# A hybrid token-mixer block on one core: PSUM copies on ScalarE, attention's end and projection reordered, S5 outputs in column halves, the first norm's chain reordered

## The chip, the cores and the metric

The kernel runs on one core of a Trainium2 chip. The metric is device time in microseconds of one execution; the figures are medians over several executions. TensorE (PE) multiplies matrices and writes to PSUM, VectorE (DVE) and ScalarE (ACT) read PSUM and SBUF and compute element by element, GpSimd (POOL) does small fills, and the SyncE queue (SP) issues most DMAs.

## The reference

One decoder layer on x of shape (1, 512, 1024). Two sub-layers, each with an RMS norm, a scale and shift made from c (adaLN), a second norm and a gated residual:

```python
mod = silu(c) @ ada_w + ada_b
sh1, sc1, gt1, sh2, sc2, gt2 = split(mod, 6)
h = rms_norm(x, pre1_w) * (1 + sc1) + sh1
gq, gk, gv, ga, gr, mq, mk, mv, mi, mf, mo, su, zg = split(h @ w_in)
y_gla = rms_norm(gla(gq, gk, gv, log_sigmoid(ga @ a2 + b) / 16)) * silu(gr)
y_ml  = sigmoid(mo) * mlstm(silu(causal_dwconv([mq, mk])), mv, mi, mf)
y_s5  = gelu(s5(su)); y_s5 = y_s5 * sigmoid(y_s5 @ glu_w + glu_b)
y = (g0 * (y_gla @ proj_gla) + g1 * (y_ml @ proj_ml) + g2 * (y_s5 @ proj_s5)) @ w_out
x = x + (1 + gt1) * rms_norm(y, post1_w)
h = rms_norm(x, pre2_w) * (1 + sc2) + sh2
a, b = split(h @ ffn_in); x = x + (1 + gt2) * rms_norm((silu(a) * b) @ ffn_out, post2_w)
```

`gla` is gated linear attention (4 heads, key width 64, value width 128), `mlstm` a matrix memory with a stabiliser, and `s5` a diagonal complex state-space layer: 32 groups of 16 channels, 64 states each, y = Re(C x_t) + D u_t.

## The kernel before

Each weight matrix is streamed once and split into a rounded part `hi` (ScalarE, `af`, L229) and a remainder `lo` (VectorE, `tt`, L220). A product is then three matmuls, hi·hi, hi·lo and lo·hi, of 128x128 weights and 512 columns (`passes`, L422 to L424; `tok_mm`, L1526 to L1528; `slab0`, L1608 to L1610). Activations lie feature by token (`hT`), 8 tiles of 128 features.

- **Head** (0 to 66 us, from L534). The engines keep the order in which it is written (`manual_schedule`). Squares of x are summed by one-column matmuls (L556); from them comes r, one factor for each token. `rd` is the identity scaled by r (L569), and `rb`, a matmul of ones with it (L573), lays r out along the free axis. adaLN comes from `ada_pe` (L485), matmuls on column tiles of 32; `evac` copies their sums (`ae`), `prep` turns them into columns `cb` (L593) and builds `hT`, then the `sweep` multiplies six 128-column slabs of the input projection over five STRIPS of features. `warm` (L541) issues matmuls whose result nobody uses.
- **Attention** (66 to 190 us). Outside the manual stretches a scheduler moves instructions of different engines, so the order written is not always the order run. `log_sig` makes decays with ACT's Abs, Exp and Ln; `level` (L1087) runs 14 times; `kdT` and `Sg` carry the state from chunk to chunk; `og` is the output, scaled by `rg` and `gr`; `to_fm` (L1200) transposes it in 16 matmuls. `fill(n)` interleaves n steps of independent projection matmuls.
- **S5** (190 to 316 us). For each of four blocks `params` builds CA, WT and M, `states` the carried states Xs, and `outputs` (L1313) multiplies M by U and CA by Xs (L1318, L1319): 128x128 weights and 64 columns, in 8 groups. The scheduler mixes DVE's pieces of one block with splits (`lo`) for the projections that fill PE.
- mLSTM (to 405 us) and the branch projections follow.
- **Out-projection** (to 562 us, manual from L1628). `half(t, h)` projects 128 tokens on 512 columns; `gated`, `normed`, `x1_out`, `second` are the second norm and the residual; `to_h2` (L1580) transposes the result; `slab0` is the first slab of the feed-forward for one token tile. The feed-forward runs to 908 us.

## Time and profile before

| | us |
|---|---|
| median of 3 runs (910.48 to 912.75) | 912.28 |
| profiled execution | 910.4 |
| its span | 908.6 |
| PE busy (98% of the span) | 888.7 |
| DVE busy (63%) | 575.7 |
| ACT busy (36%) | 331.0 |

The profiled execution is 1.8 us longer than its span and 1.9 us below the median. The share of the span is an average: the stages have different limits, so a wait of PE is looked up in its own stage. The granted clock of PE over the whole execution was 0.989 of full speed.

### The profile page before, as it was taken

How to read it: one execution, taken by the hardware profiler on the slowest of the kernel's cores; microseconds unless marked ns; L12 is line 12 of the kernel's file. 1: busy time of each engine (PE TensorE's matmuls, PEld its weight loads, DVE VectorE, ACT ScalarE, POOL GpSimd, SP SyncE). 2: the span in 40 equal slices, each digit the busy share in tenths (PEclk: the TensorE clock that was granted, in tenths of full speed). 3: DMA queues.
4: the chain of work that ended last, by engine and by line, in shares of the span. 5: the costliest groups of instructions: out<-in, count | busy, mean ns of one | idle time of the engine just before them, and what ended most of it. 6: DMA issues, size and time to landing. Idle time of an engine off the chain costs nothing.

```text
span 908.6 us, 11582 instructions
## 1 busy us (share of the span) xinstructions
PE 888.7 (98%) x4334; PEld 723.1 (80%) x4334; DVE 575.7 (63%) x1144; ACT 331.0 (36%) x512; POOL 24.9 (3%) x68
## 2 busy tenths in 40 slices
PE   9999999999989999999999989999999999999997
PEld 7667887878878878788888868888888888888885
DVE  6748999979879884966679497544433333322215
ACT  4339323431442462722334444333222332211113
POOL 2010000000000000010000000000000000000000
PEclk7999999999999999999999999999999999999999
DMA  9661341233443442345456533533333323322303
GB/s 364 251 193 47 116 128 58 82 125 111 154 139 108 121 116 93 131 127 172 153 175 226 199 140 117 185 116 117 118 126 130 113 93 116 115 93 97 113 1 139
DMA packets 52193, 120.79 MB, mean 133 GB/s; under 512 B 13797, under 2 KB 19429, under 8 KB 52137
## 3 DMA queue, kind: packets, MB, share of 16 engines
q1 hardware_dynamic: 49944, 115.92, 38.0%
q0 software_dynamic: 1040, 2.38, 1.1%
q10 hardware_dynamic: 1152, 1.75, 0.5%
q8 instruction: 34, 0.56, 0.3%
q14 instruction: 23, 0.18, 0.1%
HBM read 113.21 MB, written 6.82 MB: 132 GB/s over the span
## 4 chain that ended last, share of the span: by engine, by line
PE 77%; DVE 17%; issue 2%; ACT 2%; DMA 1%; SPq 0%; DVEq 0%; ACTq 0%
PE mm L422 16%; PE mm L423 16%; PE mm L424 16%; PE y L1527 5%; PE y L1526 5%; PE y L1528 5%; DVE lo L220 3%; PE mm L455 2%; PE mm L454 2%; PE mm L456 2%; DVE ST L1111 1%; DVE Qp L220 1%; DVE o L220 1%; DVE D L220 1%; PE ax L1318 1%
## 5 line engine op out<-in xcount | busy, mean ns | idle before, releaser
L229 ACT ACTIVATE hi<-raw 128x1024 fp32r<-128x1024 f32 (+2 forms) x157 | 151.9, 971 | 382.2 <-PE mm L423 156.2
L220 DVE TENSOR_TENSOR lo<-raw,hi 128x1024 fp32r<-128x1024 f32 (+2 forms) x157 | 174.6, 1114 | 155.6 <-ACT hi L229 155.0
L424 PE MATMUL mm<-h2hi,lo 128*128 128x512 f32 x320 | 124.6, 389 | 0.0
L423 PE MATMUL mm<-h2lo,hi 128*128 128x512 f32 x320 | 124.6, 389 | 0.0
L422 PE MATMUL mm<-h2hi,hi 128*128 128x512 f32 x320 | 124.5, 389 | 0.0
L424 PE MATMUL mm<-hT,lo 128*128 128x512 f32 x280 | 110.7, 395 | 3.1 <-DVE lo L220 3.1
L422 PE MATMUL mm<-hT,hi 128*128 128x512 f32 x280 | 112.3, 401 | 0.2 <-ACT hT L229 0.2
L423 PE MATMUL mm<-hT,hi 128*128 128x512 f32 x280 | 111.0, 396 | 0.4 <-DVE hT L226 0.4
L422 PEld LDWEIGHTS mm<-h2hi,hi 128*128 128x128 f32 x320 | 60.1, 188 | 12.5
L424 PEld LDWEIGHTS mm<-h2hi,lo 128*128 128x128 f32 x320 | 60.1, 188 | 12.4
L423 PEld LDWEIGHTS mm<-h2lo,hi 128*128 128x128 f32 x320 | 60.1, 188 | 12.3
L1528 PE MATMUL y<-hi,g 128*128 128x512 f32 x176 | 68.5, 389 | 0.0
L1527 PE MATMUL y<-lo,g 128*128 128x512 f32 x176 | 68.5, 389 | 0.0
L1526 PE MATMUL y<-hi,g 128*128 128x512 f32 x176 | 68.3, 389 | 0.0
L220 DVE TENSOR_TENSOR sg<-sg,mm 128x512 f32<-128x512 f32 x36 | 24.7, 685 | 64.8 <-PE mm L424 64.7
L422 PEld LDWEIGHTS mm<-hT,hi 128*128 128x128 f32 x280 | 53.2, 190 | 15.7 <-issue 4.0
L424 PEld LDWEIGHTS mm<-hT,lo 128*128 128x128 f32 x280 | 53.2, 190 | 14.6 <-DVE lo L220 3.5
L423 PEld LDWEIGHTS mm<-hT,hi 128*128 128x128 f32 x280 | 53.1, 190 | 11.9 <-DVE hT L226 1.2
L226 DVE SCALAR_TENSOR_TENSOR gacc<-raw,cact,gacc 128x512 f32<-128x512 f32 x56 | 41.9, 748 | 21.9 <-DMA raw<-ada 21.3
L455 PE MATMUL mm<-lo,hT 128*128 128x512 f32 x128 | 50.5, 394 | 0.4 <-DVE lo L220 0.4
L454 PE MATMUL mm<-hi,hT 128*128 128x512 f32 x128 | 49.8, 399 | 0.0
L456 PE MATMUL mm<-hi,hT 128*128 128x512 f32 x128 | 49.7, 391 | 0.0
(311 smaller groups left out, 1393.9 us busy)
## 6 DMA issues: line engine op xcount, KB each, us to landing
raw<-ada SPq DMA_DIRECT2D x48, 512.0 KB, 3.5
raw<-ffn SPq DMA_DIRECT2D x44, 512.0 KB, 3.3
raw<-wzg SPq DMA_DIRECT2D x24, 512.0 KB, 3.2
raw<-ffo SPq DMA_DIRECT2D x22, 512.0 KB, 3.3
raw<-wpr SPq DMA_DIRECT2D x24, 256.0 KB, 2.7
raw<-wout SPq DMA_DIRECT2D x8, 512.0 KB, 4.3
raw<-sweep SPq DMA_DIRECT2D x8, 384.0 KB, 8.5
xT<-xT SPq DMA_DIRECT2D x4, 512.0 KB, 5.6
```

Source lines behind the costliest of these rows:

```text
L220: e.tensor_tensor(out=o, in0=a, in1=b, op=op)
L226: dve.scalar_tensor_tensor(out=o, in0=a, scalar=s, in1=b, op0=op0, op1=op1)
L229: act.activation(out=o, in_=i, func=f, **kw)
L422: mm(ps, lhsT=whi, rhs=xhi, start=first, stop=False)
L423: mm(ps, lhsT=whi, rhs=xlo, start=False, stop=False)
L424: mm(ps, lhsT=wlo, rhs=xhi, start=False, stop=last)
L454: mm(ps[t], lhsT=xh[:, tk], rhs=hi[:, sl], start=(k == 0), stop=False)
L455: mm(ps[t], lhsT=xh[:, tk], rhs=lo[:, sl], start=False, stop=False)
L456: mm(ps[t], lhsT=xl[:, tk], rhs=hi[:, sl], start=False, stop=(k == 7))
L1526: mm(ps, lhsT=xhi, rhs=whi[:, sl], start=first, stop=False)
L1527: mm(ps, lhsT=xhi, rhs=wlo[:, sl], start=False, stop=False)
L1528: mm(ps, lhsT=xlo, rhs=whi[:, sl], start=False, stop=last)
```

## The change

The copies out of PSUM named `gk`, `su`, `kdT` and `ks`, and the first term of the causal convolution, go from VectorE to ScalarE. In attention, the output of the first token tile is multiplied before the loop that makes Sg, and `og` is scaled head by head. S5's outputs take U and Xs as 64-column weights in alternating column halves, with M and CA streamed as 128 columns; the result comes out turned round, so four transposes a block and one more copy follow. In the head, `ae` and the columns stand ahead of `rd`, `rd` is split between the two engines, the first `lo` stands behind `h`, the first strip runs all hi·hi matmuls before the others, and there are 8 more warm matmuls behind the first 18. In the out-projection `half(3, 1)` stands between `to_h2(0)` and `to_h2(1)`, and `to_h2(2)` in the middle of `slab0(1)`.

```diff
...
-WARM = (17, 1, 0, 0, 0, 0)
+WARM = (17, 1, 1, 2, 2, 3)
-SWN = ((0, 0, 2), (0, 2, 3), (2, 4, 6), (2, 4, 6))
+SWN = ((0, 1, 2), (0, 2, 3), (2, 4, 6), (2, 4, 6))
...
+        def step_hi(self):
+            i = self.done
+            t, w = self.raw.pop(i), items[i]["w"]
+            hp, lp = self.rings[3]
+            hi = hp.tile([128, w], F32R, tag="hi", name="hi")
+            lo = lp.tile([128, w], F32R, tag="lo", name="lo")
+            af(hi, t[:, 0:w], AF.Copy)
+            self.hl[i] = (hi, lo)
+            self.done += 1
+            return lambda: tt(dve, lo, t[:, 0:w], hi.bitcast(F32), OP.subtract)
...
     cp(cz[:, :, 0:1], cact.unsqueeze(2))
     wb = ax_bank()
-    def warm(n, x):
+    def warm(n, x, bank=None):
         for _ in range(n):
-            mm(wb[:, 0:128], lhsT=ones, rhs=x, start=True, stop=True)
+            mm((bank or wb)[:, 0:128], lhsT=ones, rhs=x, start=True, stop=True)
...
+    ada_sb, cbs = {}, {}
+    def evac(j):
+        n = 2 * STRIPS[j][1]
+        ada_sb[j] = slot("ae")
+        af(ada_sb[j][:, 0:n], ada_ps.pop(j)[:, 0:n], AF.Copy)
+    def columns(j):
+        cbs[j] = cb = ax_bank()
+        for i in range(2 * STRIPS[j][1] // 128):
+            sl = slice(i * 128, (i + 1) * 128)
+            mm(cb[:, i:i + 1], lhsT=ada_sb[j][:, sl], rhs=ones[:, 0:1], start=True, stop=True)
+    evac(0)
+    columns(0)
     rb = ax_bank()
     rd = slot("rd")
     for t in range(4):
         tk = slice(t * 128, (t + 1) * 128)
-        af(rd[:, tk], ident, AF.Copy, scale=r[:, t:t + 1])
+        if t % 2:
+            af(rd[:, tk], ident, AF.Copy, scale=r[:, t:t + 1])
+        else:
+            ts(dve, rd[:, tk], ident, r[:, t:t + 1], None, OP.mult)
+    for t in range(4):
+        tk = slice(t * 128, (t + 1) * 128)
         mm(rb[:, tk], lhsT=ones, rhs=rd[:, tk], start=True, stop=True)
...
+    first_lo = S.step_hi()
...
-        cb = ax_bank()
-        for i in range(2 * n):
-            sl = slice(i * 128, (i + 1) * 128)
-            mm(cb[:, i:i + 1], lhsT=ada_sb[j][:, sl], rhs=ones[:, 0:1], start=True, stop=True)
+        if j not in cbs:
+            columns(j)
+        cb = cbs.pop(j)
...
+        if j == 0:
+            first_lo()
...
+            if k == 0:
+                yield
+                xhi, xlo = hT[k]
+                for n, (w, x) in enumerate(((hi, xhi), (lo, xhi), (hi, xlo))):
+                    for b in range(6):
+                        mm(sweep_ps[b], lhsT=w[:, b * 128:(b + 1) * 128], rhs=x, start=(n == 0), stop=False)
+                    yield
+                continue
...
-            ts(dve, u, ps, w(3), P("conv_b", f), OP.mult, OP.add)
+            af(u, ps, AF.Identity, scale=w(3), bias=P("conv_b", f))
...
-            cp(u.rearrange("p (a n) -> p a n", a=8)[:, ::-1], ps.rearrange("p (n a) -> p a n", a=8))
+            af(u.rearrange("p (a n) -> p a n", a=8)[:, ::-1], ps.rearrange("p (n a) -> p a n", a=8), AF.Copy)
...
-        S.ahead(strip_w[0][-1], 0)
         prep(0)
-        warm(WARM[5], ones)
...
+                if j == 0 and n == 0:
+                    warm(WARM[5], ones, sweep_ps[0])
...
-        cp(kT[p], sweep_ps[2 + p])
+        af(kT[p], sweep_ps[2 + p], AF.Copy)
...
-        cp(kdT[p][:, 0:384], ps[:, 0:384])
+        af(kdT[p][:, 0:384], ps[:, 0:384], AF.Copy)
     FL.until("gv")
     fill(2)
...
     og = {}
     ssg, rg = st3[:, 16:32], st3[:, 32:48]
-    for t in range(4):
+    def gla_out(t):
...
+    gla_out(0)
+    for p in range(2):
...
+    for t in range(1, 4):
+        gla_out(t)
     rstd(rg, ssg, 16, 128.0)
     FL.until("gr")
-    for t in range(4):
-        for h in range(4):
+    for h in range(4):
+        for t in range(4):
...
-        cp(ks[:, 0:256], kp[:, 0:256])
+        af(ks[:, 0:256], kp[:, 0:256], AF.Copy)
...
     def outputs(b):
         ps = ax_bank()
-        for g in range(8):
-            o = ps[:, g * 64:(g + 1) * 64]
-            sl = slice(g * 128, (g + 1) * 128)
-            mm(o, lhsT=Mt[b][:, sl], rhs=U[b][:, g * 64:(g + 1) * 64], start=True, stop=False)
-            mm(o, lhsT=CA[b][:, sl], rhs=Xs[b][:, g * 64:(g + 1) * 64], start=False, stop=True)
-        Y = slot("Y")
-        af(Y, ps, AF.Gelu_apprx_tanh)
+        half = (even, odd)
+        for q in range(4):
+            for z, (x, w) in enumerate(((U[b], Mt[b]), (Xs[b], CA[b]))):
+                for h in range(2):
+                    g = 2 * q + h
+                    mm(ps[half[h], q * 128:(q + 1) * 128], lhsT=x[:, g * 64:(g + 1) * 64],
+                       rhs=w[:, g * 128:(g + 1) * 128], start=(q == 0 and z == 0), stop=(q == 3 and z == 1),
+                       tile_position=(0, 64 * h))
+        YT, Y = slot("YT"), slot("Y")
+        af(YT, ps, AF.Gelu_apprx_tanh)
+        fill(1)
+        ps = ax_bank()
+        for q in range(4):
+            pe.transpose(out=ps[:, q * 128:(q + 1) * 128], in_=YT[:, q * 128:(q + 1) * 128], identity=ident)
+        af(Y, ps, AF.Copy)
         sp.dma_start(out=ys_d[b].rearrange("a (c g) n -> (a c) (g n)", g=8), in_=Y)
-        fill(2)
+        fill(1)
...
     half(3, 0)
-    normed(2)
     to_h2(0)
     S.ahead(ffn0_i[1], 0)
+    half(3, 1)
+    normed(2)
+    S.ahead(ffn0_i[2], 0)
     x1_out(2)
-    S.ahead(ffn0_i[2], 0)
+    S.ahead(ffn0_i[3], 0)
     to_h2(1)
-    S.ahead(ffn0_i[3], 0)
-    half(3, 1)
-    second(2)
     x_tile(3, wslot, A["x"], sp)
     gated(3, yp, wslot)
+    second(2)
     slab0(0)
-    to_h2(2)
     normed(3)
     x1_out(3)
-    slab0(1)
+    slab0(1, range(4))
+    to_h2(2)
+    slab0(1, range(4, 8))
     second(3)
     slab0(2, range(4))
     slab0_g(0)
```

How the instructions stand is shown at three places. The first is PE in the head, from the adaLN matmuls to the first matmuls of the sweep; `rd`, `ae` and `hT` are as above. Before:

```order
L485 MATMUL ab<-raw,G 32x256 x8
L573 MATMUL ax<-rd,ones 128x128 x4
L593 MATMUL ax<-ones,ae 128x1 x2
L485 MATMUL ab<-raw,G 32x256 x8
L422 MATMUL mm<-hT,hi 128x512
L423 MATMUL mm<-hT,hi 128x512
L424 MATMUL mm<-hT,lo 128x512
L422 MATMUL mm<-hT,hi 128x512
```

And with the change:

```order
L497 MATMUL ab<-raw,G 32x256 x8
L553 MATMUL ax<-ones 128x128 x2
L591 MATMUL ax<-ones,ae 128x1 x2
L605 MATMUL ax<-rd,ones 128x128 x4
L497 MATMUL ab<-raw,G 32x256 x4
L553 MATMUL mm<-ones 128x128 x3
L649 MATMUL mm<-hT,hi 128x512 x4
L649 MATMUL ax<-hT,hi 128x512 x2
L497 MATMUL ab<-raw,G 32x256 x4
L649 MATMUL mm<-hT,lo 128x512 x4
```

The columns (of `ae`) now stand ahead of `rd`'s matmul, only half of the second adaLN group (L485, now L497) stands ahead of the first sweep matmul, and the hi·hi matmuls of all six slabs come first.

The second place is ACT at the end of the sweep; `t` is the argument of `log_sig`. Before:

```order
L229 ACTIVATE hi<-raw 128x1024 x3
L229 ACTIVATE gq<-mm 128x512 x2
L229 ACTIVATE t<-ax,pv 128x512
L229 ACT_TABLE_LOAD
L229 ACTIVATE t<-t 128x512
L229 ACT_TABLE_LOAD
L229 ACTIVATE t<-t 128x512
```

And with the change:

```order
L229 ACTIVATE hi<-raw 128x1024 x3
L229 ACTIVATE su<-ax 128x8x64
L229 ACTIVATE gq<-mm 128x512
L229 ACTIVATE gk<-mm 128x512
L229 ACTIVATE gq<-mm 128x512
L229 ACTIVATE gk<-mm 128x512
L229 ACTIVATE t<-ax,pv 128x512
L229 ACT_TABLE_LOAD
L229 ACTIVATE t<-t 128x512
```

Three copies (`su` and twice `gk`) have come in front of `t`, and they stay on ACT ahead of it.

The third place is DVE in the second pass of the S5 loop. CA is the table that `outputs` multiplies by Xs, `lo` the remainder of a projection weight, `gacc` a sum of adaLN rows. Before:

```order
L220 TENSOR_TENSOR CA<-o_2402,o_2403 64x4x128 x2
L220 TENSOR_TENSOR merged<-sg,mm 128x512
L226 SCALAR_TENSOR_TENSOR CA<-o_2404,o_2405 64x4x128 x2
L226 SCALAR_TENSOR_TENSOR gacc<-raw,cact,gacc 128x512
L220 TENSOR_TENSOR Xs<-x_2356,y_2357 64x4x63 x4
L220 TENSOR_TENSOR o_2418<-pw,bb 128x512
L220 TENSOR_TENSOR wp<-o_2415,o_2416 64x4x128 x2
L220 TENSOR_TENSOR lo<-raw,hi 128x1024
```

And with the change, where the long `lo` that comes last above stands between the two pairs of CA:

```order
L220 TENSOR_TENSOR o_2432<-pw,bb 128x512
L220 TENSOR_TENSOR CA<-o_2417,o_2418 64x4x128 x2
L220 TENSOR_TENSOR lo<-raw,hi 128x1024
L226 SCALAR_TENSOR_TENSOR CA<-o_2419,o_2420 64x4x128 x2
L226 SCALAR_TENSOR_TENSOR gacc<-raw,cact,gacc 128x512
L220 TENSOR_TENSOR Xs<-x_2371,y_2372 64x4x63 x4
```

That `lo` has moved ahead of the second pair of CA, `gacc`, Xs and the pieces of `wp`.

## Rows read from the trace of the kernel before

**Rows 1.** Page, busy time of the engines (us, share of the span, instructions).

```profile
PE 888.7 (98%) x4334; PEld 723.1 (80%) x4334; DVE 575.7 (63%) x1144; ACT 331.0 (36%) x512; POOL 24.9 (3%) x68
```

**Rows 2.** What PE waited for, whole span: us in total, times, longest us.

```profile
PE mm L424 <- DVE lo L220: 3.1, 1, 3.1
PE ax L1580 <- DVE xn L220: 1.9, 3, 0.7
PE ax L1200 <- DVE og L226: 1.6, 1, 1.6
...
PE ax L1177 <- DVE Sg L226: 1.1, 1, 1.1
```

**Rows 3.** Stretches: us, busy PE, PEld, DVE, ACT, POOL, PEclk, DMA share, GB/s.

```profile
5.00:12.00 7.00, 6.67 (x67) 6.17 (x66) 4.54 (x11) 4.83 (x9) 0.09 (x2) 1.00 1.03 406
12.00:25.50 13.50, 12.59 (x55) 9.06 (x48) 12.32 (x65) 6.68 (x13) 0.00 (x0) 0.50 1.03 406
...
186.00:189.40 3.40, 3.40 (x14) 2.31 (x14) 3.40 (x14) 0.39 (x1) 0.00 (x0) 0.51 0.00 0
700.00:720.00 20.00, 20.00 (x90) 16.57 (x89) 9.14 (x11) 6.23 (x9) 0.00 (x0) 1.00 0.34 118
```

**Rows 4.** Timeline of PE, head: start us, us, engine line op out<-in xcount [idle before].

```profile
13.09 2.08 PE L573 MATMUL ax<-rd,ones 128*128 128x128 f32 x8 [0.68 <-ACT rd L229]
...
17.91 0.80 PE L422 MATMUL mm<-hT,hi 128*128 128x512 f32 x1 [0.24 <-ACT hT L229]
...
24.84 0.63 PE L423 MATMUL ax<-hT,hi 128*128 128x512 f32 x1
25.27 0.56 PE L424 MATMUL ax<-hT,lo 128*128 128x512 f32 x1
...
26.46 1.07 PE L485 MATMUL ab<-raw,G 128*32 128x512 f32 x8
```

**Rows 5.** Timeline of ACT, head.

```profile
12.64 1.28 ACT L229 ACTIVATE rd<-ident,st 128x128 f32<-128x128 f32 x4 [0.84 <-DVE st L226]
```

**Rows 6.** Timeline of DVE, head.

```profile
14.95 0.96 DVE L220 TENSOR_TENSOR lo<-raw,hi 128x768 fp32r<-128x768 f32 x1 [0.26 <-ACT hi L229]
```

**Rows 7.** Groups by form, DVE: xcount, busy us, mean ns, idle before.

```profile
L232 DVE COPY su<-mm 128x512 f32<-128x512 f32 x3 | 2.1, 685 | 0.0
...
L232 DVE COPY kdT<-ax 128x384 f32<-128x384 f32 x2 | 1.1, 550 | 0.0
```

**Rows 8.** Groups by form, ACT.

```profile
L229 ACT ACTIVATE gq<-mm 128x512 f32<-128x512 f32 x2 | 1.2, 598 | 3.1 <-PE mm L424 3.0
```

**Rows 9.** Timeline of DVE after the sweep.

```profile
72.60 0.69 DVE L220 TENSOR_TENSOR g<-g,t 128x512 f32<-128x512 f32 x1 [1.49 <-ACT t L229]
```

**Rows 10.** Timeline of PE at the transposes that end attention.

```profile
185.35 4.32 PE L1200 MATMUL ax<-ident,og 128*128 128x128 f32 x16 [1.64 <-DVE og L226]
189.66 0.50 PE L422 MATMUL mm<-yhi,hi 128*128 128x512 f32 x1
```

**Rows 11.** Timeline of PE in the S5 loop.

```profile
231.50 0.39 PE L1318 MATMUL ax<-U,M 128*128 128x64 f32 x2
231.72 0.39 PE L1319 MATMUL ax<-Xs,CA 128*128 128x64 f32 x2
232.04 1.20 PE L1283 MATMUL ax<-U,WT 128*64 128x64 f32 x32
233.17 0.50 PE L422 MATMUL mm<-yhi,hi 128*128 128x512 f32 x1
```

**Rows 12.** Timeline of DVE in the S5 loop.

```profile
248.51 1.38 DVE L226 SCALAR_TENSOR_TENSOR CA<-o,o 64x512 f32<-64x512 f32 x2
...
254.34 1.23 DVE L220 TENSOR_TENSOR lo<-raw,hi 128x1024 fp32r<-128x1024 f32 x1
```

**Rows 13.** Timeline of PE in the out-projection.

```profile
525.88 1.03 PE L1580 MATMUL ax<-ident,xn 128*128 128x128 f32 x8
...
554.15 0.48 PE L1608 MATMUL ax<-hi,h2hi 128*128 128x512 f32 x1
```

More of the change, by code (lines that the diff above doesn't have):

```diff
@@ L557, in _emit @@
     af(st[:, 16:17], epsc, AF.Sqrt)
+    S.ahead(strip_a[0][-1], 0)
     warm(WARM[4], ones)
-    S.ahead(strip_a[0][-1], 0)
     w, h, u, r = (st[:, 4 * i:4 * i + 4] for i in range(4))
@@ L576, in _emit @@
     stt(cact2, r[:, 0:1].broadcast_to([128, 8]), 0.0, cact, OP.mult, OP.add)
-    ada_sb = {}
-    def evac(j):
-        n = 2 * STRIPS[j][1]
-        ada_sb[j] = slot("ae")
-        af(ada_sb[j][:, 0:n], ada_ps.pop(j)[:, 0:n], AF.Copy)
-    evac(0)
+    first_lo = S.step_hi()
     rbs = [rb]
@@ L1145, in _emit @@
         kdT[p] = slot("kdT", tag="y")
-        cp(kdT[p][:, 0:384], ps[:, 0:384])
+        af(kdT[p][:, 0:384], ps[:, 0:384], AF.Copy)
     FL.until("gv")
     fill(2)
-    for p in range(2):
-        Sg[p] = slot("Sg", tag="y")
-        for t in range(3):
-            ps = ax_bank()
-            mm(ps[:, 0:256], lhsT=kdT[p][:, t * 128:(t + 1) * 128], rhs=gv[t][:, p * 256:(p + 1) * 256],
-               start=True, stop=True)
-            for h in range(2):
-                r = slice(64 * h, 64 * h + 64)
-                o = Sg[p][r, t * 128:(t + 1) * 128]
-                if t == 0:
-                    cp(o, ps[r, h * 128:(h + 1) * 128])
-                else:
-                    stt(o, Sg[p][r, (t - 1) * 128:t * 128], ecum[p][r, t * 128 + 127:t * 128 + 128],
-                        ps[r, h * 128:(h + 1) * 128], OP.mult, OP.add)
-        fill(1)
     og = {}
     ssg, rg = st3[:, 16:32], st3[:, 32:48]
-    for t in range(4):
+    def gla_out(t):
         ps = [ax_bank(), ax_bank()]
@@ L1186, in _emit @@
         fill(1)
+    gla_out(0)
+    for p in range(2):
+        Sg[p] = slot("Sg", tag="y")
+        for t in range(3):
+            ps = ax_bank()
+            mm(ps[:, 0:256], lhsT=kdT[p][:, t * 128:(t + 1) * 128], rhs=gv[t][:, p * 256:(p + 1) * 256],
+               start=True, stop=True)
+            for h in range(2):
+                r = slice(64 * h, 64 * h + 64)
+                o = Sg[p][r, t * 128:(t + 1) * 128]
+                if t == 0:
+                    cp(o, ps[r, h * 128:(h + 1) * 128])
+                else:
+                    stt(o, Sg[p][r, (t - 1) * 128:t * 128], ecum[p][r, t * 128 + 127:t * 128 + 128],
+                        ps[r, h * 128:(h + 1) * 128], OP.mult, OP.add)
+        fill(1)
+    for t in range(1, 4):
+        gla_out(t)
     rstd(rg, ssg, 16, 128.0)
     FL.until("gr")
-    for t in range(4):
-        for h in range(4):
+    for h in range(4):
+        for t in range(4):
             sl = slice(h * 128, (h + 1) * 128)
@@ L1314, in outputs @@
         ps = ax_bank()
-        for g in range(8):
-            o = ps[:, g * 64:(g + 1) * 64]
-            sl = slice(g * 128, (g + 1) * 128)
-            mm(o, lhsT=Mt[b][:, sl], rhs=U[b][:, g * 64:(g + 1) * 64], start=True, stop=False)
-            mm(o, lhsT=CA[b][:, sl], rhs=Xs[b][:, g * 64:(g + 1) * 64], start=False, stop=True)
-        Y = slot("Y")
-        af(Y, ps, AF.Gelu_apprx_tanh)
+        half = (even, odd)
+        for q in range(4):
+            for z, (x, w) in enumerate(((U[b], Mt[b]), (Xs[b], CA[b]))):
+                for h in range(2):
+                    g = 2 * q + h
[5 more added lines that the diff above has]
+        fill(1)
+        ps = ax_bank()
+        for q in range(4):
+            pe.transpose(out=ps[:, q * 128:(q + 1) * 128], in_=YT[:, q * 128:(q + 1) * 128], identity=ident)
+        af(Y, ps, AF.Copy)
         sp.dma_start(out=ys_d[b].rearrange("a (c g) n -> (a c) (g n)", g=8), in_=Y)
-        fill(2)
+        fill(1)
     for step in range(5):
```

## The prediction

> **What bounds the kernel now.** I read the page's busy times first. TensorE (PE) is busy 888.7 us of a span of 908.6 [rows 1], so nearly all that can be won is of two kinds: time in which PE waits, and time in which it is busy but slow. The list of what PE waited for gives the first kind [rows 2]: 3.1 us for a `lo` in the S5 loop, 1.9 for `xn` in the out-projection, 1.6 for `og` and 1.1 for Sg in attention; the reader is to see that VectorE (DVE) ends all four. A window of the feed-forward gives the yardstick: 90 matmuls of 512 columns in 20 us, 0.222 us each [rows 3]. The windows of the head show the second kind: from 12 to 25.5 us the granted clock is 0.50, its lower level of 1.2 GHz, against 1.00 (2.4 GHz) from 5 to 12 us [rows 3], and two neighbouring matmuls there start 0.43 us apart [rows 4].
>
> **The head.** Before, the chain is rd, rb, columns, h, hT, first sweep matmul at 17.91 [rows 4]. `rd` is four ScalarE instructions, 1.28 us [rows 5]; two of them go to DVE, which saves about half, 0.64. The columns now run before rb. The `lo` of 0.96 us, which ended at 15.91 [rows 6], goes behind h, so h no longer waits for it: it can start at rb's end, about 15, less the 0.64. PE finished rb at 13.09 + 2.08 = 15.17 [rows 4]. So the first sweep matmul comes 0.8 (only what `rd` gives, and a little) to 1.6 us earlier; I take 1.2. Beyond that the clock decides. From 17.91 to 25.27 stand 15 matmuls of the sweep, first and last shown [rows 4], at 0.43 instead of 0.222 us; if the clock held, 15 x 0.21 = 3.1 us more would go, 4.3 with the 1.2, and with the columns that ran among them up to 5. If it falls and returns as before, nothing is added, and the 8 extra warm matmuls could delay the first strip by as much as 8 x 0.22 = 1.8 if they don't lie in a wait. They lie beside the square sums and rd, where PE waited anyway (0.68 ahead of rb [rows 4]). What holds part of a larger gain back are the loads: the DMA share from 5 to 25.5 us is 1.03 [rows 3], and their order stays, so strip 2 can't come as much earlier as strip 0. Bounds: a loss of 1 to a gain of 5. Clock granted at 1.00 up to 12 us while warm matmuls ran among the square sums speaks for part of it; I take -3.
>
> **Attention.** Four `su` copies (0.685 each, three of them by that row) and two `kdT` (0.55) leave DVE [rows 7]: inside the chain 3 x 0.685 + 2 x 0.55 = 3.2 us. Against that stands the order on ScalarE: `su` and two `gk` now run ahead of log_sig's first `t`, three copies of 0.598 [rows 8], 1.8 us later. DVE already waited 1.49 us for that `t` [rows 9], so this delay is not hidden, and the `gk` that DVE is spared gives nothing there. In the order of DVE a `lo` and a `gacc` of 512 columns now stand ahead of the `og` scaling; priced like the `su` copy of the same size they are 1.4 us. -3.2 + 1.8 + 1.4 = 0: `og` comes when it came. What goes is the pace behind it: 16 transposes took 4.32 us, each waiting for its scaling [rows 10]. Scaled head by head, only the first 8 must wait (2.16), the other 8 run after projection matmuls at transpose pace (0.11, by 1.03 us for 8 with the last one's tail [rows 13]), 0.9: -1.3. The 1.1 us wait for Sg [rows 2] is covered by the first output tile's matmuls, which need no Sg, but DVE is the slower one there, so it only moves to `og`. The clock stood at 0.51 from 186 to 189.4 us [rows 3]; there it cost nothing, since DVE paced the transposes. Now full matmuls follow after half of them: up to 3.4/2 = 1.7 us of their stretch at half rate, costing 0.8. Bounds -3 to +2.5; I take -1.
>
> **S5, the wait.** PE waits 3.1 us for a `lo` that DVE ran last in its pass, at 254.34, though the work since 248.51 had nothing to do with it [rows 12]: 5.8 us. In the new order that `lo` precedes it, so it is there 5.8 us sooner. PE arrives earlier too, by what one block of outputs saves (at most 1.6, below), so 3.1 + 1.6 = 4.7 < 5.8 and the wait goes: -3.1. What is late next is CA and Xs, 1.2 us later than before in DVE's order, the `lo` itself [rows 12]; the projection matmuls that fill PE between states and outputs hide it, least in the last block, and without them it costs that 1.2. The convolution's first term and `ks` leave DVE too. I take -3, bounds -3.1 and 0.
>
> **S5, the outputs.** Records of L1318 and L1319 start 0.11 us apart (231.50 to 231.72 is two) [rows 11]; 128 of them are 14.2 us. The new form has as many records, 64 weight columns and 128 columns streamed, in alternating halves. The trace has it in no row. The nearest is L1283, 64 weight columns and 64 streamed in the same halves: 32 in 1.13 us, 0.035 each, 0.07 a pair [rows 11]. If the weights set its pace, a pair stays at 0.07 and 64 pairs take 4.5 us; if the columns do, it doubles to 0.14 and 9.0. If the halves don't overlap at all, a record keeps the 0.11 and nothing goes, 14.2. L1283's own overlap is in the row, so I go by columns, with 8. To that come 16 transposes of 0.11 (1.8) and entering and leaving the column tiles, 0.1 each by L1283, which starts 0.32 us after 231.72 where two records take 0.22 [rows 11], 8 times: 0.8. 14.2 - 8 - 1.8 - 0.8 = 3.6; the start and the end of each block are rarely full pairs, so I take -3; bounds -6 and +3. The extra Gelu output and copy are ScalarE's, off the path. On this form the Trainium skill, "TensorEngine Tiling (Array Packing)", When to Use Tiling, says that 64 streamed columns call for exchanging the operands and two column tiles; by a full doubling 14.2 would become 7.1, and the term -4.3. The row of L1283 agrees that halves overlap, but not that columns cost nothing.
>
> **The out-projection.** From 525.88 to 554.15 PE issued 84 matmuls and 32 transposes [rows 13]: 84 x 0.222 + 32 x 0.13 (8 in 1.03) = 22.8 of 28.3, so 5.5 us are lost to `xn`, `lo`, `st` and `s`. With `half(3, 1)` between to_h2(0) and to_h2(1), 24 matmuls (5.3 us) cover the two `xn` that came late; then slab0's `lo` are due about 1.5 us sooner and DVE has them little sooner, so part comes back as a wait there, and to_h2(2) still waits for `xn` behind `gated(3)`, while to_h2(3) finds 12 more matmuls ahead. I take -2.5, bounds -4 and +1.
>
> **The sum.** -3 - 1 - 3 - 3 - 2.5 = -12.5 on 910.4, the profiled execution: 897.9. That execution lies 1.9 below the median of 912.28, so against the median it is 899.8: 900.
>
> **Rivals.**
> 1. *The waits pass on.* ScalarE's longer queue ahead of `t`, late Xs and late `lo` take the place of the waits that went, and the head's clock falls as before: head -1, attention 0, wait -1.5, outputs -3, out-projection -1 = -6.5: 906. For it: DVE ends all four waits, and what it loses inside the attention chain is 3.2 us. Against: DVE's order in the S5 loop serves the `lo` of the longest wait earlier.
> 2. *The head's clock holds and the halves overlap fully.* Head -5, outputs -6: 12.5 becomes 17.5, 895. For it: the clock at 1.00 up to 12 us; against: it fell while PE was busy 12.59 of 13.5 us [rows 3], so being busy was not enough.
> 3. *The halves take turns.* Outputs +3 instead of -3, the rest as forecast: -6.5, 906. Against: L1283.
> 4. *Slower: the clock falls in the outputs.* Half-column matmuls and transposes, in blocks of about 2 us, make the granted clock drop as at 12 us, and it stays at half for as long as there, 13.5 us; matmuls of 0.222 then take 0.43, so about 6.4 us a block, 25.6 for four: 912.28 - 12.5 + 25.6 = 925. From two blocks on (12.8) it eats the gain. For it: the 32-column tiles and one-column matmuls ahead of 12 us, the transposes at 186 us at 0.51 [rows 3]. Against: in the S5 loop L1283 and the 128-column outputs ran without it, and PE there issues 512-column matmuls on either side. The Trainium skill, "TensorE: Matmul & The Clock Gate", Part 4, says that transposes do not count as PE work for the clock; by that rule four more a block speak for this rival. The trace fits it at 186 us, yet at 189.4 the clock was back after nothing but transposes, so I give it little.
>
> **How the numbers follow.** Forecast 0.50, rival 1 0.22, rival 2 0.13, rival 3 0.08, rival 4 0.07. The forecast alone reaches from 894 to 906. The range of 889 to 910 leaves out rival 4, the poorer part of rival 1 and the far end of rival 2, some 0.14 together. About 0.3% (2.7 us) is what a measurement of this kernel can tell from no change. Within it lie the poorest of rivals 1 and 3 and rival 4 with two blocks only, 0.07; slower is rival 4 with three or four, 0.05; faster 0.88.
>
> **What would show it.** Head: first sweep matmul near 16.7, and PEclk between 12 and 25 us. Attention: transposes of `og` in two groups of 8, the first after a wait of about 1.6 us, and ACT's first `t` near 69.8. S5: no wait of PE at 250 to 256; outputs of about 2 us a block instead of 3.6, PEclk 1.00. Out-projection: to_h2(3) done near 551 instead of 554.15. The prediction is wrong if PE's wait list still holds a `lo` or Xs of over 2 us in the S5 loop, if a pair of half-column records takes 0.22 us, or if PEclk falls in the S5 loop.

## The result, and the profile after

The changed kernel took **917.0 us** (median, 915.12 to 920.11), the kernel before on the same chip 911.38 (909.29 to 912.75): ratio **1.0066, 95% interval 1.0044 to 1.0088**. That is 5.6 us slower; 12.3 faster was forecast (900, range 889 to 910). The profiled execution has a span of 915.3 us against 908.6. Of the runs below, executions that ran throughout at a lower granted clock (0.75 to 0.84: one of c_kdt, three of d_kdt0) or took 2 to 5 ms (one each of o_reg, d_kdt0 and before) are left out of the times, and no profile of such an execution is read.

Marks that both kernels have say where: the first `ga` matmul behind the sweep starts at 66.77 before and 66.38 after, `to_h2(0)` at 525.88 [rows 13] and 531.88, the first matmul behind `to_h2(3)` at 554.15 [rows 13] and 560.87. So in these two executions the head won 0.4, the stretch from attention to the branch projections lost 6.4, the out-projection 0.7, and behind it nothing changed.

The page's busy line of after answers to [rows 1]: PE is busy 2.0 us longer, DVE 7.2 us shorter, ACT 9.9 longer.

```profile
PE 890.7 (97%) x4366; PEld 720.2 (79%) x4366; DVE 568.5 (62%) x1130; ACT 340.9 (37%) x530; POOL 25.0 (3%) x68
```

What PE waited for in the changed kernel, whole span (us in total, times, longest), answers to [rows 2]:

```profile
PE ax L1239 <- DVE og L226: 4.6, 1, 4.6
PE mm L434 <- ACT hi L229: 3.1, 1, 3.1
PE ax L1308 <- DVE wp L220: 1.4, 1, 1.4
PE mm L467 <- DVE lo L220: 1.1, 1, 1.1
...
PE mm L436 <- DVE lo L220: 0.9, 1, 0.9
PE ax L1629 <- DVE s L220: 0.9, 1, 0.9
...
PE ax L1629 <- DVE xn L220: 0.6, 1, 0.6
```

Of the four waits of [rows 2] the one for Sg is gone, that for `xn` has shrunk from 1.9 to 0.6 and that for `lo` from 3.1 to 0.9, but `og` has grown from 1.6 to 4.6, and `hi` (3.1) and `wp` (1.4) are new. From 66 to 345 us PE waited 6.4 us before and 11.6 after. In the out-projection (L1629, L1657, L1658) six waits add to 4.7, against 4.1 before.

DVE tells why, by one row of its own waits between the sweep and 260 us. First before, then after:

```profile
DVE lo L220 <- ACT hi L229: 0.2, 1, 0.2
```

```profile
DVE lo L220 <- ACT hi L229: 11.5, 4, 3.7
```

DVE was relieved of 10.0 us of work between the sweep's end and the S5 wait (busy 175.2 before, 165.2 after) and stood idle 28.6 instead of 14.4 us. It waits for the rounded weights `hi`, which ScalarE makes when a load has landed and a buffer is free.

**Head.** PE's timeline of after, to be read beside [rows 4]:

```profile
15.25 2.05 PE L605 MATMUL ax<-rd,ones 128*128 128x128 f32 x8
...
19.55 1.97 PE L649 MATMUL mm<-hT,hi 128*128 128x512 f32 x4
...
25.93 1.07 PE L497 MATMUL ab<-raw,G 128*32 128x512 f32 x8
```

The first sweep matmul is 1.6 us later than in [rows 4]: the matmul of `rd` stands behind `ae`, its columns and warm matmuls and starts 2.2 later. The first adaLN matmuls of 512 columns are 0.5 us earlier all the same (25.93 against 26.46): from 12 to 25.5 us PE no longer stops (13.50 us busy against 12.59 [rows 3]), and its clock there was 0.66 in this execution, not 0.50. The trace does not say how much each gave. The windows (columns as in [rows 3]):

```profile
12.00:25.50 13.50, 13.50 (x75) 9.77 (x68) 10.12 (x56) 4.29 (x9) 0.00 (x0) 0.66 1.03 406
257.30:263.40 6.10, 5.15 (x11) 3.67 (x12) 5.93 (x11) 0.01 (x1) 0.31 (x1) 0.50 0.24 89
```

**Attention.** ACT in the changed kernel after the sweep, and then DVE, which waits for its `t` (answers to [rows 9]):

```profile
66.35 0.60 ACT L229 ACTIVATE su<-ax 128x512 f32<-128x512 f32 x1 [6.97 <-PE ax L436]
...
68.75 0.73 ACT L229 ACTIVATE t<-ax,pv 128x512 f32<-128x512 f32 x1
```

```profile
69.51 0.75 DVE L223 TENSOR_SCALAR g<-ax,pv 128x512 f32<-128x512 f32 x1 [1.36 <-ACT t L229]
73.39 0.69 DVE L220 TENSOR_TENSOR g<-g,t 128x512 f32<-128x512 f32 x1 [3.14 <-ACT t L229]
```

The wait of 1.49 us [rows 9] has become 1.36 and 3.14, but `g` itself comes only 0.8 later (73.39 against 72.60), as ACT's first `t` does (68.75 against 67.99). At attention's end PE has, against [rows 10]:

```profile
164.82 0.71 PE L1192 MATMUL ax<-Sg,qE 64*128 64x128 f32 x4
...
187.93 2.31 PE L1239 MATMUL ax<-ident,og 128*128 128x128 f32 x8 [4.57 <-DVE og L226]
```

**S5.** The timeline of PE in the second pass, against [rows 11]:

```profile
234.05 0.48 PE L1361 MATMUL ax<-CA,Xs 128*64 128x128 f32 x3
...
239.60 0.60 PE L1369 MATMUL ax<-ident,YT 128*128 128x128 f32 x4
240.13 1.20 PE L1322 MATMUL ax<-U,WT 128*64 128x64 f32 x32
...
257.36 0.79 PE L434 MATMUL mm<-yhi,hi 128*128 128x512 f32 x1 [3.10 <-ACT hi L229]
...
259.47 0.80 PE L436 MATMUL mm<-hT,lo 128*128 128x512 f32 x1 [0.90 <-DVE lo L220]
260.06 0.63 PE L434 MATMUL mm<-hT,hi 128*128 128x512 f32 x1
```

Before, the states (L1283, now L1322) stood right behind the outputs, at 232.04 [rows 11]; now the fill matmuls and the four transposes stand between, and they start at 240.13.

The 3.10 us can be followed back link by link: PE waits for a `hi`, ACT for the load of its `raw`, SyncE for DVE to free the buffer, DVE for a `hi` before (at 245.72), and that for PE or for another load, which stood in SyncE's queue behind the small DMAs of `ks`. Changed kernel; ACT, then DVE, then SyncE's issues:

```profile
245.72 0.63 ACT L229 ACTIVATE hi<-raw 128x512 fp32r<-128x512 f32 x1 [4.88 <-PE mm L436]
...
256.68 0.63 ACT L229 ACTIVATE hi<-raw 128x512 fp32r<-128x512 f32 x1 [2.77 <-DMA raw<-wpr]
```

```profile
232.21 0.37 DVE L226 SCALAR_TENSOR_TENSOR ks<-cs,pv,ks 128x16 f32<-128x16 f32 x2
...
241.37 0.69 DVE L220 TENSOR_TENSOR x<-ax,ph 128x512 f32<-128x512 f32 x1 [0.83 <-PE ax L1322]
...
246.38 0.69 DVE L220 TENSOR_TENSOR lo<-raw,hi 128x512 fp32r<-128x512 f32 x1 [3.72 <-ACT hi L229]
...
253.11 0.74 DVE L226 SCALAR_TENSOR_TENSOR gacc<-raw,cact,gacc 128x512 f32<-128x512 f32 x1
```

```profile
232.74 1.78 SPq L1301 DMA_DIRECT2D kd_d<-ks  x4
238.65 3.62 SPq L1312 DMA_DIRECT2D M<-kd_d  x8
242.37 0.38 SPq L319 DMA_DIRECT2D raw<-wpr  x1
...
253.88 0.34 SPq L319 DMA_DIRECT2D raw<-wpr  x1
```

And before, SyncE's issues of the same DMAs:

```profile
230.17 1.73 SPq L1262 DMA_DIRECT2D kd_d<-ks  x4
233.79 3.62 SPq L1273 DMA_DIRECT2D M<-kd_d  x8
...
237.98 0.38 SPq L319 DMA_DIRECT2D raw<-wpr  x1
...
245.91 0.33 SPq L319 DMA_DIRECT2D raw<-wpr  x1
```

`ks` is ready 2.4 us later (232.21 against 229.77), because all of DVE's stream is: `merged`, `wp` and two `lo` of projection weights stand ahead of it in both kernels, and they start at 228.18 instead of 224.61; 2.6 us of that came in with `og`, whose transposes start at 187.93 instead of 185.35. The writes of `kd_d` go out 2.6 later, the eight loads of M behind them 4.9 later (SyncE waited 3.9 us for the last write), and the weight load queued behind those 4.4 later (242.37). It landed 3.2 us after its issue, at 245.6. But the line of its `hi` at 245.72 names PE: the matmul that it waited for ended at 245.64, so the two waits ended together, and the trace doesn't show that an earlier load alone would have brought this `hi` sooner. DVE stops for that weight 3.72 us until 246.38, so its `gacc` ends at 253.85; only then is a buffer free (SyncE waited 4.0 us for it), the next `raw` goes out at 253.88 (245.91 before), and its `hi` at 256.68 is what PE waits for.

**Sum of the 6.4 us from 66 to 526.** PE's waits grew by 5.2. Matmuls behind the waits ran at half clock: 11 in the window from 257.3 at 0.43 instead of 0.227 us apart, 2.2, and about 1 more behind the og transposes. The outputs gave back 3.5 (below) and the `og` transposes 1.4 (4.31 before; 1.97 and 0.96 after). That is 3.5; some 2.9 stay without a name.

### The profile page after: what moved, and what is told of

The parts are those of the page before. It is cut to its first block, busy times and chain, and to the rows that moved or that the text cites. A ratio compares the mean times of both kernels' runs of the same rounds, so it can differ in the third digit from the quotient of the medians.

```text
span 915.3 us, 11672 instructions
## 1 busy us (share of the span) xinstructions
PE 890.7 (97%) x4366; PEld 720.2 (79%) x4366; DVE 568.5 (62%) x1130; ACT 340.9 (37%) x530; POOL 25.0 (3%) x68
## 4 chain that ended last, share of the span: by engine, by line
PE 83%; DVE 10%; ACT 3%; DMA 2%; issue 2%; SPq 1%; DVEq 0%; POOL 0%; ACTq 0%; POOLq 0%
PE mm L434 16%; PE mm L436 16%; PE mm L435 16%; PE y L1575 5%; PE y L1576 5%; PE y L1577 5%; PE mm L467 2%; PE mm L468 2%; PE mm L466 2%; DVE lo L220 2%; PE ax L1141 1%; DVE o L220 1%; PE ab L497 1%; PE ax L1361 1%; PE ax L553 1%
## 5 line engine op out<-in xcount | busy, mean ns | idle before, releaser
L434 PE MATMUL mm<-hT,hi 128*128 128x512 f32 x276 | 110.4, 400 | 0.1
L435 PE MATMUL mm<-hT,hi 128*128 128x512 f32 x276 | 109.5, 397 | 0.4 <-DVE hT L226 0.4
L436 PEld LDWEIGHTS mm<-h2hi,lo 128*128 128x128 f32 x320 | 60.1, 188 | 12.3
```

What stands on the lines that cost most here:

```text
L434: mm(ps, lhsT=whi, rhs=xhi, start=first, stop=False)
L435: mm(ps, lhsT=whi, rhs=xlo, start=False, stop=False)
L436: mm(ps, lhsT=wlo, rhs=xhi, start=False, stop=last)
```

## The experiments

The kernel before was measured beside each group of runs: 911.2 to 911.6 us, in the last group 910.9. "With X undone" is the changed kernel with one part as before; "X alone" is the kernel before with one part changed.

### Undoing parts, and two parts alone

Outputs as before (u_out):

```diff
-    mm(ps[half[h], ...], lhsT=x[...], rhs=w[...], ..., tile_position=(0, 64 * h))
-    pe.transpose(out=ps[...], in_=YT[...], identity=ident)
+    mm(o, lhsT=Mt[b][:, sl], rhs=U[b][...]); mm(o, lhsT=CA[b][:, sl], rhs=Xs[b][...])
```

> The changed kernel with S5's outputs as before (128x128 weights, 64 columns, no transposes of the result, fill of 2). Theory A (in the changed kernel the outputs' four transposes, and the 22 projection matmuls in front of them, stand on TensorE ahead of the next block's states, so VectorE's chain starts some 5 us later in each pass and TensorE waits for what it makes last; the form itself saves about 3.5 us): the S5 loop goes back to before, about 4 us less, 913 us, no half clock at 257 to 263 us, and a wait for a lo of about 3 us near 255. Theory B (the copies moved to ScalarE, ks and conv in S5, hold up the splits on ScalarE; the form of the outputs saves its 3.5 us): 917 + 3.5 = 920.5 us, and the wait for ScalarE's hi stays.

Measured 915.5, ratio 1.0055 (1.0036 to 1.0074): between the times of the two theories. The loss stays without the new outputs, so they are not needed for it, nor is a clock that falls in them. But PE's waits for `og` (4.57) and `lo` (4.97) and the half clock behind them stay too, against theory A.

The four transposes behind the next block's states (a_defer):

```diff
         if step >= 1:
             states(step - 1)
+        if step >= 2:
+            turn(step - 2)      # transposes, copy and store of that block
```

> The changed kernel with the four transposes of a block's outputs (and the copy and store behind them) put after the next block's states instead of before them; the fill of 2 stands behind the outputs as before. Nothing else differs. Theory A: states follow the outputs within 4 to 14 projection matmuls instead of 22 and the transposes, VectorE starts 2 to 4 us sooner in each pass, the waits of 3.1 and 0.9 us and the half clock behind them go: 5 to 7 us less, 910 to 912 us. Theory B (ScalarE's copies): no change, 916 to 918 us.

914.0, 1.0037 (1.0021 to 1.0053). The states start early again, but DVE then has `merged` and a `lo` ahead of their product, and PE's one wait for `lo` is 5.1. Neither theory gave this time.

Attention undone (u_att: copies of `su`, `gk`, `kdT`, the order of the output tiles, the scaling by heads):

```diff
-        af(kdT[p][:, 0:384], ps[:, 0:384], AF.Copy)
+        cp(kdT[p][:, 0:384], ps[:, 0:384])
```

> The changed kernel with attention as before: su, gk and kdT copied by VectorE, Sg made before the first output tile, og scaled tile by tile. Theory C (the copies in front of log_sig's first Abs on ScalarE, and the output of the first tile before Sg, delay og by 2.6 us and let the clock fall there): about 2 to 2.5 us less, 914.5 to 915 us; TensorE's wait for og back to about 1.6 us. Rival D (og is late because VectorE's chain is as long as before, whoever copies): 916.5 to 917.5 us, wait for og still 4 us.

922.56, 1.0122 (1.0104 to 1.0139): up, not down. What PE waited for there, 66 to 345 us:

```profile
PE mm L436 <- DVE lo L220: 9.2, 2, 6.5
PE mm L466 <- DVE conv L226: 3.1, 1, 3.1
PE ax L1235 <- DVE og L226: 1.6, 1, 1.6
```

The og wait is back at 1.6 as before, and the S5 loop pays 6.5 us for one `lo`. Theories C and D both expected less. The attention edits cost time in attention, and PE waits less behind attention with them than without: the parts do not add.

The new outputs alone (o_out), put into the kernel before:

```diff
-    mm(o, lhsT=Mt[b][:, sl], rhs=U[b][...]); mm(o, lhsT=CA[b][:, sl], rhs=Xs[b][...])
+    mm(ps[half[h], ...], lhsT=x[:, g * 64:(g + 1) * 64], rhs=w[:, g * 128:(g + 1) * 128], ..., tile_position=(0, 64 * h))
```

> The kernel before with the new S5 outputs alone (column halves, transposes, fill 1 and 1). Theory A: TensorE saves about 3.5 us of work and loses 7 or more by the late states: 3 to 4 us slower than before, 914 to 915.5 us. Theory B (the loss in the S5 loop comes from the copies on ScalarE, which this kernel doesn't have): 3 to 3.5 us faster than before, 908 us.

915.96, 1.0057 (1.0044 to 1.007), slower, near theory A's 914 to 915.5. Undoing the same part (u_out) still saved nothing clear (1.0055 against 1.0066). Its S5 wait for `lo` is split (1.5 the longest), and 3.6 us of waiting for `wp` have come in.

### Which edits, and is it DVE's work?

Two levels of attention left out (x_level):

```diff
-            level(l, p, n % NQ)
+            if l != 3:
+                level(l, p, n % NQ)
```

> The kernel before with two of the 14 levels of attention left out (level 3 of both halves; that part of the computation is missing). It takes about 2.8 us of VectorE a level away (0.75 + 0.84 + 0.43 + 0.77), 5.6 in all, and 0.9 us of TensorE (8 matmuls of 0.11). Theory E (from the end of the sweep to the lo of 256 us VectorE's stream is the bound, and TensorE's waits for Sg, og and that lo only show where it catches up): 4 to 5.5 us faster, 906 to 907.5 us, with those three waits (5.8 us in before) nearly gone. Rival F (each wait is of its own making, set by the order around it): 1 us faster, 910.5 us.

913.99, 1.0034 (1.0021 to 1.0047): slower, with some 5.6 us of DVE's work taken out. Neither expectation held. Less work on DVE is no gain here: PE's wait for `og` is 4.9 in this kernel, though the output tiles stand in the order of before.

The five kinds of copies on ACT, alone (o_copies), and undone (u_copies):

```diff
-        cp(kT[p], sweep_ps[2 + p])
+        af(kT[p], sweep_ps[2 + p], AF.Copy)
```

> The kernel before with the copies alone: gk, su, kdT, ks and the first term of the convolution made by ScalarE. Theory G (VectorE loses 10 us of work but waits as much or more for ScalarE, whose queue now holds log_sig's Abs and the splits behind copies): 0 to 4 us slower than before, 911.5 to 915.5 us; VectorE's idle time between 66 and 256 us rises from about 11 us by 10 or more. Rival H (the copies help by what they take from VectorE, and the loss comes from the S5 outputs and the order in attention): 3 to 5 us faster, 907 to 908.5 us.

915.51, 1.0056 (1.0038 to 1.0075).

> The changed kernel with all five kinds of copies back on VectorE. Theory G: 2 to 5 us less than the changed kernel (917), 912 to 915 us. Rival H: 3 to 5 us more, 920 to 922 us.

921.16, 1.0115 (1.01 to 1.013). The first fits theory G, the second the time of rival H: alone the copies cost 5 us, and taken out of the change it is 4 slower still. Again not a sum.

The order of the output tiles and the scaling by heads, alone (o_gla):

```diff
+    gla_out(0)
+    for p in range(2):
+        ...
+    for t in range(1, 4):
+        gla_out(t)
```

> The kernel before with the order in attention alone: the first output tile before Sg, og scaled head by head. Under theory E it changes nothing that VectorE does, so within 1 us of before, 910.5 to 912.5 us, the wait for Sg moved to og or to the lo of 256 us. Rival C (this order is what makes og late): 2 us slower, 913.5 us.

917.41, 1.0071 (1.0059 to 1.0083). What PE waited for, 66 to 345 us:

```profile
PE mm L424 <- DVE lo L220: 5.0, 1, 5.0
PE ax L1204 <- DVE og L226: 4.8, 1, 4.8
```

The og wait of the changed kernel comes with this edit: 4.6 to 4.8 in every kernel that has it, 1.3 to 1.6 in o_copies, u_att and o_out, which measure without it. It is not the only way to such a wait: x_level has 4.9 without the edit. The time is 4 us above rival C's; PE's wait for `lo` is 5.0 here too.

### Parts that leave the order alone

Head alone (o_head), out-projection alone (o_reg), scaling by heads alone (c_hm); a line or two of each:

```diff
+    evac(0)
+    columns(0)
     rb = ax_bank()
...
     to_h2(0)
+    half(3, 1)
...
-    for t in range(4):
-        for h in range(4):
+    for h in range(4):
+        for t in range(4):
```

> The kernel before with the new head alone (columns and ae ahead of rd, rd split, lo behind h, first strip by hi and lo, 8 more warm matmuls). The order of the three engines behind the head stays nearly as it was. Theory E (VectorE's stream is the bound from the sweep to 256 us, and starts when the sweep ends): what the sweep gains arrives at the end, 0.5 to 2 us faster, 909.5 to 911 us. Rival: warm matmuls and loads eat it, within 0.5 us of before.

> The kernel before with the new order of the out-projection alone; nothing else moves. By the trace of the changed kernel (5.6 us lost there before, 6.6 after): 0.4 to 1 us slower, 912 us. By the prediction: 2.5 us faster, 908.9 us.

> The kernel before with og scaled head by head alone. VectorE's order changes in 4 places, TensorE's in 16, the loads' in none. Theory I (what costs is VectorE's order, and here it is kept): the prediction's price holds, 0.5 to 1.5 us faster or, where VectorE is the bound behind it, no change: 910 to 911.5 us. Rival (this edit makes og and the splits behind it late by itself): 2 us slower or more.

910.7, 0.9991 (0.9983 to 1.0); 911.2, 0.9999 (0.9991 to 1.0008); 909.5, 0.9986 (0.9975 to 0.9996). None loses. In all three the waits of 66 to 345 us are those of before to 0.1 us, but for a `lo` of 3.6 in o_head.

The `kdT` copies alone: both (c_kdt), that of the first half (d_kdt0), that of the second (d_kdt1).

```diff
-        cp(kdT[p][:, 0:384], ps[:, 0:384])
+        (af(kdT[p][:, 0:384], ps[:, 0:384], AF.Copy) if p == 0 else cp(kdT[p][:, 0:384], ps[:, 0:384]))
```

> The kernel before with the two kdT copies alone on ScalarE: 1.1 us less for VectorE, and its order changes in 52 places, that of the loads in 10. Theory I: slower by 2 to 5 us, 913 to 916 us, with 5 us or more of new waits in VectorE's stream between 140 and 256 us. Rival (the edits themselves cost): two copies of 0.55 us can't cost that, within 1 us of before.

> The kernel before with one kdT copy, that of p = 0, on ScalarE. VectorE's order changes in 50 places into the S5 loop, the loads' in 10. Theory I (the order decides): 2 to 4 us slower, 913.5 to 915.5 us. Rival (one copy of 0.55 us can't matter): within 0.5 us of before.

> The kernel before with the other kdT copy, that of p = 1, on ScalarE. VectorE's order changes in 16 places, all in attention; in the S5 loop and for the loads it stays. Theory I: within 1 us of before, 910.5 to 912 us. Rival (a kdT copy on ScalarE costs by itself): as much slower as p = 0.

914.0, 1.0031 (1.0018 to 1.0044); 912.4, 1.001 (0.9995 to 1.0026), less than expected and undecided; 911.6, 1.0 (0.999 to 1.001). Only the times of the first two are used. One instruction of 0.55 us, moved to ACT, shifts DVE's order against before in 50 places (d_kdt0; both copies 52), or in 16, all in attention (d_kdt1); the second costs nothing. That the first costs something is not shown; both together cost 2.8 us.

### What is left when the harmless parts are put together

Head and scaling by heads (d_headhm: the diffs of o_head and c_hm); the same with the new outputs, transposes deferred (d_headhmod: those of o_out and a_defer too); the first with the out-projection's order (f_hhr: that of o_reg too).

> The kernel before with the new head and with og scaled head by head, the two parts that alone kept the order and did not lose (0.9991 and 0.9986 of before). Theory I: they add up, 0.9977, about 909.2 us. Rival (behind the bound one hides the other): 0.9986 or more.

> The kernel of the third run with the new S5 outputs too, their transposes behind the next states. TensorE has 3.5 us less to do, half of it behind the wait at 256 us. By the work: 1.5 to 3 us faster than the third run, 906 to 908 us. Theory I: VectorE's order in S5 changes in some 35 places again, so 0 to 4 us slower than the third run, 909 to 913 us.

> The kernel before with three parts of the change together, each of which kept the order of the S5 loop alone: the head, the head-by-head scaling of og, and the out-projection's order. Theory I: the sum of the three ratios measured alone or in pairs (0.9982 for head and scaling, 0.9999 for the out-projection), so 0.997 to 0.999, 908.6 to 910.6; og's wait 1.64, the S5 loop's lo 3.1 to 3.6. Rival (even parts that are harmless alone add up to a loss when put together): 1.001 or more.

d_headhm 909.83, 0.9982 (0.997 to 0.9995); f_hhr 909.76, 0.9981 (0.9969 to 0.9993): the furthest ahead of before, by 1.6 to 1.7 us by the ratio. They beat both kernels. Since PE's waits from 66 to 345 us are those of before in both, the gain lies elsewhere, in part perhaps in the clock: over its executions f_hhr was granted 0.9935 on average, before 0.9896. d_headhmod 910.02, 0.9992 (0.9978 to 1.0005), is in the range of theory I and short of the 906 to 908 that its work promised: in its profile, its slowest execution (913.86), PE's wait for `lo` is 5.0, which takes 1.9 of what the outputs give.

### Work taken away with the order kept

Four multiplications of 0.69 us ahead of the og scaling left out (e_nogr):

```diff
-        tt(dve, gr[t], gr[t], GL["normw"], OP.mult)
```

> The kernel before without the four multiplications of gr by its weight vector on DVE (4 x 0.69 = 2.8 us; that factor is left out of the result). Nothing else is edited, and DVE's order differs from before in 8 places, all inside attention; SyncE's in none. Theory I (the order decides): the work that is taken away stands ahead of the og scaling, so PE's wait of 1.64 us for og goes or shrinks, the S5 loop keeps its order, its wait for lo stays at 3.0 to 3.2 us, and the time is 1 to 2.7 us shorter, 908.7 to 910.5. Rival (any change of DVE's work in attention only passes on): the S5 wait grows by what og's wait loses, and the time stays within 0.7 us of before, 910.7 to 912. Third possibility, as in x_level: slower by 1 or more, which would refute the theory, since the order is kept.

911.07, 0.9996 (0.9981 to 1.0011): within the rival's range and outside theory I's 908.7 to 910.5, though the interval, 1.7 us faster to 1.0 slower, covers theory I's smallest gains. DVE and then PE in its trace:

```profile
184.26 0.87 DVE L226 SCALAR_TENSOR_TENSOR og<-og,st,gr 128x128 f32<-128x128 f32 x3
```

```profile
256.72 0.50 PE L424 MATMUL mm<-hT,lo 128*128 128x512 f32 x1 [3.06 <-DVE lo L220]
```

The scaling starts 0.7 us earlier than at 184.95; of 2.76 us of work 2.1 became idle time of DVE further up. PE came 0.7 earlier too, so the og wait stayed at 1.7 and the `lo` wait at 3.06: neither wait moved as theory I or the rival had it. In this execution the clock was also at 0.50 from 189.4 to 192.8 us, where it was 0.99 before, so the 0.7 us won at `og` had gone before the S5 wait, which ends at 256.72 instead of 255.62. Most of the work taken from DVE came back as its idle time even with the order kept; so it is not the order alone that eats a gain.

### The runs side by side

PE's waits from 66 to 345 us (summed from its timeline), DVE's waits of `lo` for `hi` to 260 us, and the places where SyncE's and DVE's order differ from before (names compared without numbers; DVE's count depends on how moved pieces are matched and is to be read as a size):

| kernel | ratio | PE waits | lo for hi | SyncE, DVE places |
|---|---|---|---|---|
| f_hhr | 0.9981 | 6.4 | 1.3 | 2, 30 |
| d_headhm | 0.9982 | 6.4 | 0.2 | 0, 25 |
| c_hm | 0.9986 | 6.4 | 0.9 | 0, 4 |
| o_head | 0.9991 | 7.0 | 0.2 | 0, 23 |
| d_headhmod | 0.9992 | 8.4 | 1.9 | 8, 60 |
| e_nogr | 0.9996 | 6.4 | 0.8 | 0, 8 |
| o_reg | 0.9999 | 6.4 | 0.2 | 2, 5 |
| d_kdt1 | 1.0000 | 5.9 | 0.4 | 0, 16 |
| d_kdt0 | 1.0010 | - | - | 10, 50 |
| c_kdt | 1.0031 | - | - | 10, 52 |
| x_level | 1.0034 | 10.5 | 3.9 | 12, 74 |
| a_defer | 1.0037 | 11.0 | 7.0 | 12, 109 |
| u_out | 1.0055 | 10.9 | 5.1 | 13, 95 |
| o_copies | 1.0056 | 8.6 | 3.0 | 15, 75 |
| o_out | 1.0057 | 9.8 | 4.7 | 8, 41 |
| after | 1.0066 | 11.6 | 11.5 | 12, 110 |
| o_gla | 1.0071 | 11.1 | 4.4 | 3, 33 |
| u_copies | 1.0115 | 13.6 | 10.2 | 13, 97 |
| u_att | 1.0122 | 17.1 | 7.3 | 14, 74 |

All kernels that keep SyncE's order to two places or fewer are level or ahead; of those that change it in more, all are behind but d_headhmod and d_kdt0, which are undecided, and PE's waits are longer in all whose profile is read. The size of the loss does not follow the count: o_gla loses most of the single parts with three places. No run changed SyncE's order by itself, so this is a pattern and not a cause shown.

## Why the prediction was wrong, step by step

**The step that failed is "S5, the wait"** (-3): that the `lo` of 3.1 us, standing earlier in DVE's order, "is there 5.8 us sooner". Its place in the order was read rightly, its time was not. I counted DVE's stream as if DVE ran through it without stopping, as it did before (0.2 us of waiting for `hi`). In the new order it stops 11.5 us for `hi`, one of these stops (3.72) right in that pass; the products of the states, ahead of that `lo` in DVE's order, start 8.1 us later (241.37 against 233.28), because on PE the fill and four transposes now stand in front of the states; and the stream had come 2.6 us late out of attention. So the `lo` at 258.19 comes 3.9 later than the one at 254.34 [rows 12], not 5.8 earlier. In place of 3.1 us stand 3.10, 1.4 and 0.9. The trace of before had the links in SyncE's view, which I read for no term: loads that wait for DVE to free `raw`, and weight loads queued behind M's.

**Attention** (-1, bounds -3 to +2.5). The `lo` and `gacc` ahead of the scaling, the three copies ahead of `t` and the two groups of 8 transposes came as written; the transposes gave the -1.3 (4.31 us before, 2.93 after) and the half clock behind them cost about 1, as priced. ACT's `t` came 0.8 us later, not 1.8. What failed is "`og` comes when it came": its scaling starts at 187.53 instead of 184.95. Missed was that the second Sg matmuls run 2 to 3 us later with the first tile's output pulled ahead (8 in two groups at 164.82 and 165.88, before in one at 162.84), and DVE stops 1.80 us there for a `hi`: the og wait became 4.57 instead of staying near 1.6. o_gla and u_copies show the long wait with that edit, u_att and o_copies the short one without it; c_hm, with the scaling by heads alone, has 1.64, so it is the order of the tiles.

**The outputs** (-3) are right. 128 records, 64 of each operand pair, start 8.78 us in sum apart, 0.14 a pair, against 14.24; the 16 transposes of `YT` take 1.94: -3.5. Two halves overlap, and the pair of 128 columns takes twice the 0.07 of L1283's pair of 64, so here the columns set the pace. (With 7.1 for the records the sum of this part would be -4.5, not the -4.3 written.) Rivals 3 and 4 fall; the clock at half from 257.3 follows a wait of 3.10 and not an outputs block, and u_out, without the new outputs, loses as well.

**The head** (-3). PE's own work in front of `rb` grew (first sweep matmul 19.55 instead of the 16.7 forecast). Even in the four profiles in which the clock held with this head, that matmul came at 17.56 to 18.24, against 17.91 before. What failed is that `h` "can start at rb's end": in d_headhm `rb` ends at 15.29, but `h` starts at 16.68, behind small pieces `w` in DVE's order, and PE waits for `hT`. PE, then DVE:

```profile
14.15 1.14 PE L605 MATMUL ax<-rd,ones 128*128 128x128 f32 x8
...
18.24 1.20 PE L649 MATMUL mm<-hT,hi 128*128 128x512 f32 x4 [1.51 <-ACT hT L229]
```

```profile
15.96 0.80 DVE L226 SCALAR_TENSOR_TENSOR w<-w 128x16 f32<-128x16 f32 x4
16.68 0.75 DVE L226 SCALAR_TENSOR_TENSOR h<-xT,g1c,ax 128x512 f32<-128x512 f32 x1
```

The clock from 12 to 25.5 us differs from one execution to the next with either head, but not alike: in the nine profiles read with the old head it is 0.50 to 0.79, in the nine with the new one 0.66 to 1.00, four of them at 1.00 (d_headhm, f_hhr, u_copies, u_att). So rival 2's "the clock holds" came true in some executions of kernels with this head and not in the one profiled of the change; the first `ga` matmul starts at 65.8 us on average with the old head and at 64.8 with the new one. That the head does it is likely but not shown, as these kernels differ elsewhere too. Measured alone: -0.8 (0 to -1.5), within the bounds of -5 to +1, not at -3.

**The out-projection** (-2.5): 5.5 us of loss were read, the two `xn` did go, but six waits of 0.6 to 0.9 came instead; 28.27 became 28.99, and alone the edit measures 0.9999. The sentence that "part comes back as a wait there" was right and should have been all of it.

**Rival 1, the waits pass on,** is what happened, with its mechanism and its prime witness (DVE ends the waits), yet its price of 906 was a forecast of less gain and never of a loss: I let a passed-on wait be at most as long as the one removed. Here 6.4 us became 11.6. The range of 889 to 910 and 0.05 for slower were wrong for that reason.

**What is shown and what stays open.** Shown: 5.2 us of the loss are waits of PE from 66 to 345 us; the changed kernel's og wait comes with the output tiles' order; seven kernels that leave SyncE's order nearly alone lose nothing clear of the noise. Argued, not shown: that the S5 waits come from DVE's new order through SyncE's queue. It rests on one chain in one trace, with a link that PE and a load ended together, and on the table's pattern. Open: why the order of one run costs 8 us and of another 4, since no run had the changed kernel's work in the order of before; 2.9 us of the 6.4; and part of the loss in the profiled execution is clock, which differs between executions.

## What to carry to other kernels

When a scheduler orders the work, a small edit is priced by the order it leads to: look up where each engine's stream and SyncE's queue have moved, and price a moved instruction by the time its inputs arrive, not by its place. Work taken from an engine that waits for others can come back as its idle time: here 10.0 us less work on DVE became 14.2 us more of standing idle. Measure parts alone, and keep those that leave the order alone: two of them together gave 1.6 us (0.9982, 0.997 to 0.9995), while the whole lost 5.6.
